# Embedding lookup with positions: indices transposed on VectorE, positions sent without a gate, GpSimd as leader, fewer quarter stores

## The chip, the core and the metric

The kernel runs on one core of a Trainium2 chip. The metric is device time in microseconds (us), the median of several runs. A profile of one execution stands beside it: its span runs from the first to the last instruction of the program, and is some 4 us shorter than the measured time.

The engines that matter here are GpSimd (POOL in the profile), which issues the gathers; VectorE (DVE), which adds; ScalarE (ACT), whose queue issues all plain loads and stores; and the 16 DMA engines that move the data of both. TensorE (PE) has a small part in the kernel before.

## The reference

Each of 32 sequences of 512 indices picks rows of 512 float32 (2 KB) from a table of 50,000 rows, and the row's position vector is added:

```python
batch, seq_len, vocab_size, d_model = 32, 512, 50000, 512

def reference(indices, embedding_table, position_embed):
    token_embed = embedding_table[indices]
    return (token_embed + position_embed).astype(np.float32)
```

The kernel gets the indices as 64-bit integers and uses the lower 32-bit word of each. It reads 33.55 MB of table rows and writes 33.55 MB of output.

## The kernel before

A sequence is laid on 128 partitions with K = 4 positions on each: position 4p + k is on partition p. A gather fetches, for one (sequence b, k), one row for each of 128 partitions, which is 256 KB. There are 128 gathers, and each has one add and a share of a store. Twenty-three slots of SBUF hold a sequence each, so that the first nine are used twice.

```python
P, K, SLOTS, LANES, FIRST, Q = 128, 4, 23, 10, 4, 32     # (shortened)
...
half = K // 2
order = [(b, k) for h in range(2) for b in range(FIRST)
         for k in range(h * half, (h + 1) * half)]
order += [(b, k) for b in range(FIRST, B) for k in range(K)]
stores = []
for g, (b, k) in enumerate(order):
    if (b <= 1 and k < half) or b == B - 1:
        stores.append((g + 1, b, k, 1))
    elif k % half == half - 1:
        stores.append((g + 1, b, k + 1 - half, half))
```

So the first four sequences are gathered in two passes, k = 0 and 1 first, k = 2 and 3 later. A store is a half sequence (512 KB of output), or a quarter (256 KB) for the first halves of sequences 0 and 1 and for all of sequence 31.

ScalarE's queue loads the indices and positions. The indices of sequence 0, of sequences 1 to 3, and of all sequences come in three loads; the second half of the positions is issued only after the first half has landed:

```python
with tc.tile_critical(sync_engine=nc.vector.engine, no_gpsimd_drain=True):


    nc.scalar.dma_start(out=idx0[:, 0, :], in_=idx_first[:, 0, :]).then_inc(
        s_first, 16
    )
    load_pos(0)
    nc.scalar.dma_start(out=idx0[:, 1:, :], in_=idx_first[:, 1:, :]).then_inc(
        s_next, 16
    )
    nc.scalar.dma_start(
        out=idx_raw[:], in_=idx_rows.rearrange("r (s w) -> r s w", w=2)
    ).then_inc(s_raw, 16)
    nc.scalar.wait_ge(s_pos[0], 16)
    load_pos(1)
```

GpSimd builds an identity matrix, waits for the indices of sequence 0 and issues all gathers. From gather 16 on (sequence 4) it takes the indices from `idx_t`, which the preparation below makes. At most LANES = 10 gathers are in flight:

```python
    nc.gpsimd.affine_select(
        out=ident[:], in_=nc.const_aps.tensor(1.0, [P, P], f32),
        pattern=[[-1, P]], compare_op=mybir.AluOpType.is_equal, fill=0.0,
        base=0, channel_multiplier=1,
    ).then_inc(s_prep, 1)
    nc.gpsimd.wait_ge(s_first, 16)
    for g, (b, k) in enumerate(order):
        if g == half:
            nc.gpsimd.wait_ge(s_next, 16)
        if g == FIRST * K:
            nc.gpsimd.wait_ge(s_prep, 2 + K + J)
        if b == SLOTS and k == 0:
            done = sum(1 for x in stores if x[1] in reused)
            nc.gpsimd.wait_ge(s_out, 16 * done)
        if b < FIRST:
            where = idx0[:, b, 2 * k : 2 * k + 1]
        else:
            where = idx_t[:, k, b : b + 1]
        ins = nc.gpsimd.indirect_dma_start(
            out=slots[b % SLOTS][:, k, :],
            out_offset=None,
            in_=table,
            in_offset=bass.IndirectOffsetOnAxis(ap=where, axis=0),
        ).then_inc(s_gather[g % LANES], 16)
        if g >= LANES:
            ins._wait_ge(s_gather[g % LANES], rounds(g - LANES))
    nc.gpsimd.drain()
```

The indices of all sequences lie in memory with 128 consecutive positions to a row of `idx_raw`; they are needed with position 4p + k on partition p. VectorE casts them to float32, TensorE turns them with four transposes into PSUM, and VectorE casts them back with four copies. These stand among the adds, ahead of adds 7 and 9. The positions are copied to PSUM, so that an add has one operand there:

```python
    nc.tensor.wait_ge(s_prep, 2)
    for k in range(K):
        nc.tensor.transpose(
            turned[:, k].rearrange("p b j -> p (b j)"), idx_f[:, :, k], ident[:]
        ).then_inc(s_prep, 1)


    for g, (b, k) in enumerate(order):
        if g == 7:
            nc.vector.tensor_copy(
                out=idx_f[:].rearrange("r p k -> r (p k)"), in_=idx_raw[:, :, 0]
            )._wait_ge(s_raw, 16).then_inc(s_prep, 1)
        if g == 9:
            nc.vector.wait_ge(s_prep, 2 + K)
            for j in range(J):
                nc.vector.tensor_copy(
                    out=idx_t[j * Q : (j + 1) * Q, :, :], in_=turned[:, :, :, j]
                ).then_inc(s_prep, 1)
        if b == 0:
            nc.vector.tensor_copy(out=pos_ps[:, k, :], in_=pos_sb[:, k, :])._wait_ge(
                s_pos[k // half], 16
            ).then_inc(s_ps, 1)
            nc.vector.wait_ge(s_ps, k + 1)
        part = slots[b % SLOTS][:, k, :]
        nc.vector.tensor_tensor(
            out=part, in0=part, in1=pos_ps[:, k, :], op=add
        )._wait_ge(s_gather[g % LANES], rounds(g)).then_inc(s_add, 1)


    rest = 0
    for adds, b, at, n in stores:
        done = s_out if b in reused else s_rest
        rest += b not in reused
        nc.scalar.dma_start(
            out=out_rows[b][:, at : at + n, :],
            in_=slots[b % SLOTS][:, at : at + n, :],
        )._wait_ge(s_add, adds).then_inc(done, 16)
tc.no_sync_barrier()
nc.scalar.wait_ge(s_rest, nc.scalar.to_reg(16 * rest))
```

Of the kernel before, what the change touches and what calls it, by code (L numbers as in the profile page):

```python
# [7 lines left out]
P = 128  # L8
K = 4
SLOTS = 23  # L10
LANES = 10
FIRST = 4
Q = 32


@with_exitstack
def kernel(
    ctx: ExitStack,
    tc: tile.TileContext,
    indices: bass.AP,  # L20
    embedding_table: bass.AP,
    position_embed: bass.AP,
    out: bass.AP,
):

    nc = tc.nc
    f32 = mybir.dt.float32
    i32 = mybir.dt.int32
    add = mybir.AluOpType.add

    B, S = indices.shape
    V, D = embedding_table.shape
    assert S == P * K and B == 32
    assert V < (1 << 24), "an index passes through float32"
    J = P // Q  # L40


    idx_words = indices.bitcast(i32)
    idx_first = idx_words[0:FIRST].rearrange("b (p w) -> p b w", p=P)
    idx_rows = idx_words.rearrange("b (j w) -> (b j) w", j=J)
    out_rows = out.rearrange("b (p k) d -> b p k d", k=K)
    pos_rows = position_embed.rearrange("(p k) d -> p k d", k=K)
    table = embedding_table[:, :]

    def sbuf(name, shape, dtype):  # L50
        return ctx.enter_context(tc.tile_pool(name="p_" + name, bufs=1)).tile(
            shape, dtype, name=name
        )

    def psum(name, shape, dtype):
        pool = tc.tile_pool(name="p_" + name, bufs=1, space=bass.MemoryType.PSUM)
        return ctx.enter_context(pool).tile(shape, dtype, name=name)

    idx0 = sbuf("idx0", [P, FIRST, 2 * K], i32)
    idx_raw = sbuf("idx_raw", [P, Q * K, 2], i32)  # L60
    ident = sbuf("ident", [P, P], f32)
    idx_f = sbuf("idx_f", [P, Q, K], f32)
    idx_t = sbuf("idx_t", [P, K, B], i32)
    pos_sb = sbuf("pos_sb", [P, K, D], f32)
    slots = [sbuf(f"slot{n}", [P, K, D], f32) for n in range(SLOTS)]
    turned = psum("turned", [Q, K, B, J], f32)
    pos_ps = psum("pos_ps", [P, K, D], f32)


# [4 lines that stand above are left out]
    order += [(b, k) for b in range(FIRST, B) for k in range(K)]  # L74
    stores = []
    for g, (b, k) in enumerate(order):
        if (b <= 1 and k < half) or b == B - 1:
            stores.append((g + 1, b, k, 1))
        elif k % half == half - 1:
            stores.append((g + 1, b, k + 1 - half, half))  # L80

    sem = tc.alloc_semaphore
    s_first, s_next, s_raw = sem("s_first"), sem("s_next"), sem("s_raw")
    s_pos = [sem(f"s_pos{h}") for h in range(2)]
    s_gather = [sem(f"s_gather{n}") for n in range(LANES)]

    reused = range(B - SLOTS)
    s_out, s_rest = sem("s_out"), sem("s_rest")

    s_prep, s_ps, s_add = sem("s_prep"), sem("s_ps"), sem("s_add")  # L90

    def rounds(g):
        return 16 * (g // LANES + 1)

    def load_pos(h):
        part = slice(h * half, (h + 1) * half)
        nc.scalar.dma_start(out=pos_sb[:, part, :], in_=pos_rows[:, part, :]).then_inc(
            s_pos[h], 16
        )

    with tc.tile_critical(sync_engine=nc.vector.engine, no_gpsimd_drain=True):  # L101


        nc.scalar.dma_start(out=idx0[:, 0, :], in_=idx_first[:, 0, :]).then_inc(
            s_first, 16
        )
        load_pos(0)
        nc.scalar.dma_start(out=idx0[:, 1:, :], in_=idx_first[:, 1:, :]).then_inc(
            s_next, 16
        )  # L110
        nc.scalar.dma_start(
            out=idx_raw[:], in_=idx_rows.rearrange("r (s w) -> r s w", w=2)
        ).then_inc(s_raw, 16)
        nc.scalar.wait_ge(s_pos[0], 16)
        load_pos(1)


        nc.gpsimd.affine_select(  # L118
            out=ident[:], in_=nc.const_aps.tensor(1.0, [P, P], f32),
            pattern=[[-1, P]], compare_op=mybir.AluOpType.is_equal, fill=0.0,  # L120
            base=0, channel_multiplier=1,
        ).then_inc(s_prep, 1)
        nc.gpsimd.wait_ge(s_first, 16)
        for g, (b, k) in enumerate(order):
            if g == half:
                nc.gpsimd.wait_ge(s_next, 16)
            if g == FIRST * K:
                nc.gpsimd.wait_ge(s_prep, 2 + K + J)
            if b == SLOTS and k == 0:
                done = sum(1 for x in stores if x[1] in reused)  # L130
                nc.gpsimd.wait_ge(s_out, 16 * done)
            if b < FIRST:
                where = idx0[:, b, 2 * k : 2 * k + 1]
            else:
                where = idx_t[:, k, b : b + 1]
            ins = nc.gpsimd.indirect_dma_start(  # L136
# [7 lines that stand above are left out]
        nc.gpsimd.drain()  # L144


        nc.tensor.wait_ge(s_prep, 2)
        for k in range(K):
            nc.tensor.transpose(  # L149
                turned[:, k].rearrange("p b j -> p (b j)"), idx_f[:, :, k], ident[:]  # L150
            ).then_inc(s_prep, 1)


        for g, (b, k) in enumerate(order):
            if g == 7:
                nc.vector.tensor_copy(  # L156
                    out=idx_f[:].rearrange("r p k -> r (p k)"), in_=idx_raw[:, :, 0]
                )._wait_ge(s_raw, 16).then_inc(s_prep, 1)
            if g == 9:
                nc.vector.wait_ge(s_prep, 2 + K)  # L160
                for j in range(J):
                    nc.vector.tensor_copy(  # L162
                        out=idx_t[j * Q : (j + 1) * Q, :, :], in_=turned[:, :, :, j]
                    ).then_inc(s_prep, 1)
            if b == 0:
                nc.vector.tensor_copy(out=pos_ps[:, k, :], in_=pos_sb[:, k, :])._wait_ge(  # L166
                    s_pos[k // half], 16
# [18 lines that stand above are left out]
# [30 lines left out]
```

## Time and profile before

| | before |
|---|---|
| median of 3 runs | 181.71 us (181.65 to 181.85) |
| span of the profile | 178.1 us |
| GpSimd busy | 121.8 us (68%), 133 instructions |
| VectorE busy | 91.4 us (51%), 137 instructions |
| TensorE busy | 1.0 us |
| moved by DMA | 68.34 MB, mean 384 GB/s |
| gathers, as a share of 16 DMA engines | 48.1% |
| loads and stores, likewise | 48.6% |
| one gather issued by GpSimd | 0.95 us |
| one add, 128x512 float32 | 687 ns |

Busy time is time in which an engine works; the rest it waits or has nothing to do. In a chain of waits, "issue" is time in which an engine waited for nothing that the profile shows. "Releaser" is what ended a wait. A DMA's landing is the moment its completion is seen. The share of the DMA engines is the mean over 16 of them, and packets that overlap count in full, so that it can be a little over 1.

The profile lists, for one gather on GpSimd, only its issue; when its data is there is read from the add that waits for it.

### The profile page before, as it was taken

The numbers are of one execution on the slowest core, as the hardware profiler recorded it, in microseconds if no ns is written. First come the engines' busy times: TensorE is split into PE (matmuls) and PEld (weight loads), VectorE is DVE, ScalarE is ACT, GpSimd is POOL, SyncE is SP. The second block draws the span as 40 slices with busy tenths as digits, with TensorE's granted clock in tenths as the row PEclk, the third lists the DMA queues.
The fourth block names the chain that finished last, engine by engine and source line by source line (L and its number), as shares of the span: only waits on it lengthen the run. The fifth ranks groups of instructions, "written<-read, shape, count | busy, mean of one in ns | idle before, by whom it ended". The sixth has DMA issues, their size and how long they took to land.

```text
span 178.1 us, 415 instructions
## 1 busy us (share of the span) xinstructions
PE 1.0 (1%) x4; PEld 0.4 (0%) x4; DVE 91.4 (51%) x137; POOL 121.8 (68%) x133
## 2 busy tenths in 40 slices
PE   0000100000000000000000000000000000000000
PEld 0000000000000000000000000000000000000000
DVE  0445973455556555555556455555556555554510
POOL 3777777777777777777777777777777777774000
DMA  4899999999999999999999999999999999999960
GB/s 122 234 329 359 375 378 364 385 410 413 416 416 419 419 419 420 419 420 419 419 420 420 419 419 418 419 418 419 420 419 420 418 420 420 420 419 421 417 258 0
DMA packets 21011, 68.34 MB, mean 384 GB/s; under 512 B 3728, under 2 KB 3856, under 8 KB 21008
## 3 DMA queue, kind: packets, MB, share of 16 engines
q10 hardware_dynamic: 10768, 34.76, 48.6%
q0 software_dynamic: 10240, 33.56, 48.1%
q14 instruction: 3, 0.02, 0.0%
HBM read 34.75 MB, written 33.55 MB: 384 GB/s over the span
## 4 chain that ended last, share of the span: by engine, by line
POOL 65%; issue 23%; DMA 5%; DVE 2%; ACTq 0%; DVEq 0%
POOL slot L136 65%; DMA slot<-in_embedding_table_dram,idx_t 4%; DVE slot L171 2%; DMA idx<-in_indices_dram 1%; ACTq L211 0%; DVEq L101 0%
## 5 line engine op out<-in xcount | busy, mean ns | idle before, releaser
L136 POOL DMA_INDIRECT slot<-in_embedding_table_dram,idx_t x112 | 106.0, 946 | 34.1 <-issue 34.1
L171 DVE TENSOR_TENSOR slot<-slot,pos_ps 128x512 f32<-128x512 f32 x128 | 87.7, 687 | 73.8 <-issue 57.8
L136 POOL DMA_INDIRECT slot<-in_embedding_table_dram,idx x16 | 15.3, 958 | 6.0 <-issue 4.6
L166 DVE COPY pos_ps<-pos_sb 128x512 f32<-128x512 f32 x4 | 2.7, 685 | 4.9 <-DMA pos_sb<-in_position_embed_dram 4.9
L162 DVE CAST idx_t<-turned 32x128 int32<-32x128 f32 x4 | 1.1, 280 | 0.1
L149 PE MATMUL turned<-ident,idx_f 128*32 128x128 f32 x4 | 1.0, 413 | 17.6 <-issue 17.6
L118 POOL TENSOR_SCALAR_AFFINE_SELECT ident<-const-float32-1.0 128x128 f32<-128x128 f32 x1 | 0.3, 282 | 0.7 <-DVEq L101 0.7
L149 PEld LDWEIGHTS turned<-ident,idx_f 128*32 128x32 f32 x4 | 0.4, 131 | 17.7 <-issue 17.6
L200 POOL MEMSET const-float32-0.0<- 128x1 f32 x1 | 0.1, 99 | 0.3 <-issue 0.3
L156 DVE CAST idx_f<-idx_raw 128x128 f32<-128x128 int32 x1 | 0.2, 220 | 0.0
L200 POOL MEMSET const-uint8-127<- 128x1 uint8 x1 | 0.1, 116 | 0.0
L200 POOL MEMSET const-bfloat16-1.0<- 128x1 bf16 x1 | 0.1, 110 | 0.0
L200 POOL MEMSET const-float32-1.0<- 128x1 f32 x1 | 0.1, 102 | 0.0
## 6 DMA issues: line engine op xcount, KB each, us to landing
out_dram<-slot ACTq DMA_DIRECT2D x60, 512.0 KB
out_dram<-slot ACTq DMA_DIRECT2D x8, 256.0 KB
slot<-in_embedding_table_dram,idx_t POOLq DMA_INDIRECT x112
pos_sb<-in_position_embed_dram ACTq DMA_DIRECT2D x2, 512.0 KB, 4.7
slot<-in_embedding_table_dram,idx POOLq DMA_INDIRECT x16
idx_raw<-in_indices_dram ACTq DMA_DIRECT2D x1, 128.0 KB
idx<-in_indices_dram ACTq DMA_DIRECT2D x1, 4.0 KB, 1.6
idx<-in_indices_dram ACTq DMA_DIRECT2D x1, 12.0 KB
```

The lines of the kernel that those rows point to most:

```text
L118: nc.gpsimd.affine_select(out=ident[:], in_=nc.const_aps.tensor(1.0, [P, P], f32), pattern=[[-1, P]], compare_op=mybir.AluOpType.is_equal, ...
L136: ins = nc.gpsimd.indirect_dma_start(out=slots[b % SLOTS][:, k, :], out_offset=None, in_=table, in_offset=bass.IndirectOffsetOnAxis(ap=whe ...
L149: nc.tensor.transpose(turned[:, k].rearrange("p b j -> p (b j)"), idx_f[:, :, k], ident[:]).then_inc(s_prep, 1)
L156: nc.vector.tensor_copy(out=idx_f[:].rearrange("r p k -> r (p k)"), in_=idx_raw[:, :, 0])._wait_ge(s_raw, 16).then_inc(s_prep, 1)
L162: nc.vector.tensor_copy(out=idx_t[j * Q : (j + 1) * Q, :, :], in_=turned[:, :, :, j]).then_inc(s_prep, 1)
L166: nc.vector.tensor_copy(out=pos_ps[:, k, :], in_=pos_sb[:, k, :])._wait_ge(s_pos[k // half], 16).then_inc(s_ps, 1)
L171: nc.vector.tensor_tensor(out=part, in0=part, in1=pos_ps[:, k, :], op=add)._wait_ge(s_gather[g % LANES], rounds(g)).then_inc(s_add, 1)
L200: nc = _bacc.Bacc("TRN2", target_bir_lowering=False, num_devices=1)
```

## The change

It has five parts.

1. The indices are transposed by VectorE itself, in squares of 32, as the first thing that VectorE does. The identity, the casts and TensorE's transposes go. For this the indices are loaded in four parts, each to 32 partitions, so that after the transposition of each square a position is on its partition.
2. `idx0` holds the indices of sequence 0 alone; the load for sequences 1 to 3 goes. GpSimd takes the transposed indices from gather 2 on (`g == half`), where before it took them from gather 16.
3. The second half of the positions is issued without waiting for the first.
4. The critical section is led by GpSimd instead of VectorE. The leader signals the other engines at its start and collects them at its end.
5. Quarter stores remain only for the first half of sequence 0 and the second half of sequence 31: there are 4 instead of 8, and 66 stores instead of 68.

It is meant to make the preparation of the indices shorter and simpler, to have the positions sooner, and to have fewer small transfers.

The diff, cut to its core:

```diff
-    idx_first = idx_words[0:FIRST].rearrange("b (p w) -> p b w", p=P)
-    idx_rows = idx_words.rearrange("b (j w) -> (b j) w", j=J)
+    idx_first = idx_words[0].rearrange("(p w) -> p w", p=P)
+    idx_rows = idx_words.rearrange("b (j w) -> b j w", j=J)
...
-    idx0 = sbuf("idx0", [P, FIRST, 2 * K], i32)
-    idx_raw = sbuf("idx_raw", [P, Q * K, 2], i32)
-    ident = sbuf("ident", [P, P], f32)
-    idx_f = sbuf("idx_f", [P, Q, K], f32)
+    idx0 = sbuf("idx0", [P, 2 * K], i32)
+    idx_raw = sbuf("idx_raw", [P, 2 * Q * K], i32)
...
-        if (b <= 1 and k < half) or b == B - 1:
+        if (b == 0 and k < half) or (b == B - 1 and k >= half):
             stores.append((g + 1, b, k, 1))
...
-    with tc.tile_critical(sync_engine=nc.vector.engine, no_gpsimd_drain=True):
+    with tc.tile_critical(sync_engine=nc.gpsimd.engine, no_gpsimd_drain=True):
-        nc.scalar.dma_start(out=idx0[:, 0, :], in_=idx_first[:, 0, :]).then_inc(
-            s_first, 16
-        )
+        nc.scalar.dma_start(out=idx0[:, :], in_=idx_first).then_inc(s_first, 16)
         load_pos(0)
-        nc.scalar.dma_start(out=idx0[:, 1:, :], in_=idx_first[:, 1:, :]).then_inc(
-            s_next, 16
-        )
-        nc.scalar.dma_start(
-            out=idx_raw[:], in_=idx_rows.rearrange("r (s w) -> r s w", w=2)
-        ).then_inc(s_raw, 16)
-        nc.scalar.wait_ge(s_pos[0], 16)
+        for j in range(J):
+            nc.scalar.dma_start(
+                out=idx_raw[j * B : (j + 1) * B, :], in_=idx_rows[:, j, :]
+            ).then_inc(s_raw, 16)
         load_pos(1)
...
-        nc.gpsimd.affine_select(
...
         nc.gpsimd.wait_ge(s_first, 16)
         for g, (b, k) in enumerate(order):
             if g == half:
-                nc.gpsimd.wait_ge(s_next, 16)
-            if g == FIRST * K:
-                nc.gpsimd.wait_ge(s_prep, 2 + K + J)
+                nc.gpsimd.wait_ge(s_idx, 1)
...
-            if b < FIRST:
-                where = idx0[:, b, 2 * k : 2 * k + 1]
+            if g < half:
+                where = idx0[:, 2 * k : 2 * k + 1]
             else:
                 where = idx_t[:, k, b : b + 1]
...
-        nc.tensor.wait_ge(s_prep, 2)
-        for k in range(K):
-            nc.tensor.transpose(
...
+        nc.vector.transpose(
+            out=idx_t[:],
+            in_=idx_raw[:].rearrange("r (q k w) -> r k q w", k=K, w=2)[:, :, :, 0],
+        )._wait_ge(s_raw, 16 * J).then_inc(s_idx, 1)
         for g, (b, k) in enumerate(order):
-            if g == 7:
-                nc.vector.tensor_copy(
-                    out=idx_f[:].rearrange("r p k -> r (p k)"), in_=idx_raw[:, :, 0]
-                )._wait_ge(s_raw, 16).then_inc(s_prep, 1)
-            if g == 9:
-                nc.vector.wait_ge(s_prep, 2 + K)
-                for j in range(J):
-                    nc.vector.tensor_copy(
-                        out=idx_t[j * Q : (j + 1) * Q, :, :], in_=turned[:, :, :, j]
-                    ).then_inc(s_prep, 1)
```

More of the change, by code (lines that the diff above doesn't have):

```diff
@@ L38 @@
     assert S == P * K and B == 32
-    assert V < (1 << 24), "an index passes through float32"
     J = P // Q
+    assert B == Q, "indices are turned in squares of 32"
     idx_words = indices.bitcast(i32)
-    idx_first = idx_words[0:FIRST].rearrange("b (p w) -> p b w", p=P)
-    idx_rows = idx_words.rearrange("b (j w) -> (b j) w", j=J)
+    idx_first = idx_words[0].rearrange("(p w) -> p w", p=P)
+    idx_rows = idx_words.rearrange("b (j w) -> b j w", j=J)
     out_rows = out.rearrange("b (p k) d -> b p k d", k=K)
@@ L65 @@
     slots = [sbuf(f"slot{n}", [P, K, D], f32) for n in range(SLOTS)]
-    turned = psum("turned", [Q, K, B, J], f32)
     pos_ps = psum("pos_ps", [P, K, D], f32)
@@ L82 @@
     sem = tc.alloc_semaphore
-    s_first, s_next, s_raw = sem("s_first"), sem("s_next"), sem("s_raw")
+    s_first, s_raw, s_idx = sem("s_first"), sem("s_raw"), sem("s_idx")
     s_pos = [sem(f"s_pos{h}") for h in range(2)]
@@ L88 @@
     s_out, s_rest = sem("s_out"), sem("s_rest")
-    s_prep, s_ps, s_add = sem("s_prep"), sem("s_ps"), sem("s_add")
+    s_ps, s_add = sem("s_ps"), sem("s_add")
     def rounds(g):
@@ L99, in load_pos @@
         )
-    with tc.tile_critical(sync_engine=nc.vector.engine, no_gpsimd_drain=True):
-        nc.scalar.dma_start(out=idx0[:, 0, :], in_=idx_first[:, 0, :]).then_inc(
-            s_first, 16
-        )
+    with tc.tile_critical(sync_engine=nc.gpsimd.engine, no_gpsimd_drain=True):
+        nc.scalar.dma_start(out=idx0[:, :], in_=idx_first).then_inc(s_first, 16)
         load_pos(0)
-        nc.scalar.dma_start(out=idx0[:, 1:, :], in_=idx_first[:, 1:, :]).then_inc(
-            s_next, 16
-        )
-        nc.scalar.dma_start(
-            out=idx_raw[:], in_=idx_rows.rearrange("r (s w) -> r s w", w=2)
-        ).then_inc(s_raw, 16)
-        nc.scalar.wait_ge(s_pos[0], 16)
-        load_pos(1)
-        nc.gpsimd.affine_select(
-            out=ident[:], in_=nc.const_aps.tensor(1.0, [P, P], f32),
-            pattern=[[-1, P]], compare_op=mybir.AluOpType.is_equal, fill=0.0,
-            base=0, channel_multiplier=1,
-        ).then_inc(s_prep, 1)
+        for j in range(J):
+            nc.scalar.dma_start(
+                out=idx_raw[j * B : (j + 1) * B, :], in_=idx_rows[:, j, :]
+            ).then_inc(s_raw, 16)
+        load_pos(1)
         nc.gpsimd.wait_ge(s_first, 16)
@@ L144 @@
         nc.gpsimd.drain()
-        nc.tensor.wait_ge(s_prep, 2)
-        for k in range(K):
-            nc.tensor.transpose(
-                turned[:, k].rearrange("p b j -> p (b j)"), idx_f[:, :, k], ident[:]
-            ).then_inc(s_prep, 1)
-        for g, (b, k) in enumerate(order):
-            if g == 7:
-                nc.vector.tensor_copy(
-                    out=idx_f[:].rearrange("r p k -> r (p k)"), in_=idx_raw[:, :, 0]
-                )._wait_ge(s_raw, 16).then_inc(s_prep, 1)
-            if g == 9:
-                nc.vector.wait_ge(s_prep, 2 + K)
-                for j in range(J):
-                    nc.vector.tensor_copy(
-                        out=idx_t[j * Q : (j + 1) * Q, :, :], in_=turned[:, :, :, j]
-                    ).then_inc(s_prep, 1)
+        nc.vector.transpose(
+            out=idx_t[:],
+            in_=idx_raw[:].rearrange("r (q k w) -> r k q w", k=K, w=2)[:, :, :, 0],
+        )._wait_ge(s_raw, 16 * J).then_inc(s_idx, 1)
+        for g, (b, k) in enumerate(order):
             if b == 0:
```

## The prediction

> **What bounds the kernel now.** I first read the page's share of busy time (GpSimd 68%, VectorE 51%) and its DMA row, then the same span cut into stretches, because a kernel that starts empty and ends empty has stages with different limits. In these rows the last three numbers are the granted clock, the mean busy share of the 16 DMA engines and GB/s.
>
> ```profile
> 2.00:4.00 2.00, 0.00 (x0) 0.00 (x0) 0.00 (x0) 1.11 (x1) 1.00 0.72 215
> 4.00:6.00 2.00, 0.00 (x0) 0.00 (x0) 0.69 (x1) 1.39 (x3) 1.00 0.94 250
> 6.00:10.00 4.00, 0.00 (x0) 0.00 (x0) 1.29 (x2) 3.09 (x4) 1.00 0.85 223
> 10.00:15.00 5.00, 0.00 (x0) 0.00 (x0) 2.81 (x5) 3.78 (x5) 1.00 0.95 356
> 15.00:40.00 25.00, 1.04 (x4) 0.43 (x4) 14.82 (x26) 18.91 (x21) 1.00 1.01 381
> 40.00:160.00 120.00, 0.00 (x0) 0.00 (x0) 65.87 (x97) 90.75 (x97) 1.00 1.03 418
> 160.00:170.00 10.00, 0.00 (x0) 0.00 (x0) 5.64 (x9) 2.28 (x3) 1.00 1.03 418
> ...
> 171.00:173.10 2.10, 0.00 (x0) 0.00 (x0) 0.00 (x0) 0.00 (x0) 1.00 0.53 203
> 173.10:178.10 5.00, 0.00 (x0) 0.00 (x0) 0.00 (x0) 0.00 (x0) 1.00 0.00 0
> ```
>
> From 40 to 170 us the DMA engines are full: share 1.03, 418 GB/s, also after GpSimd has issued its last gather at 162.9 us. So the transfers are a bound. GpSimd is a second one of the same size. The chain of waits shows it issuing a gather every 1.25 us (0.95 us of work and 0.30 us of "issue"), from the second gather on and without one longer gap:
>
> ```profile
> 4.33 0.95 POOL slot L136
> 5.28 0.30 issue
> 5.59 0.95 POOL slot L136
> 6.54 0.30 issue
> ```
>
> 128 such steps are 160 us, from 2.89 to 162.9. A step asks for 256 KB of gather and 256 KB of store, 524,288 bytes in 1.25 us or 419 GB/s, which is what the engines move. The time from a gather's end on GpSimd to its add on VectorE tells how far the DMA engines are behind: 2.6 us for the first gather (4.03 to 6.67 us in the timeline), 6.7 us for the last (162.89 to 169.59). That queue of some 4 us was built in the first 40 us and is never worked off. So a gain can only come from the two ends: DMA engines that idle early (shares 0.72 to 0.95 up to 15 us), and the last microseconds, where the share is 0.53. The 5 us after the last byte are program end.
>
> **What the skill says.** The Trainium skill, "DMA: Bandwidth & Descriptors", section "Queues, rings and completion order", says that each DMA engine takes its queues in turn, a packet at a time. The trace agrees: gathers (q0) and the other transfers (q10) hold 48.1% and 48.6%. So positions sent early share with gathers and don't shut them out. "VectorE: DVE Perf Modes", section "The three transpose paths", says that VectorE transposes 32x32 blocks, 311 ns for 128x128 bf16. No transpose of this kind runs before, so the trace can't confirm it; my estimate for 128x128 int32 is 0.25 to 0.4 us, from that figure and the cast of equal shape at 220 ns in this profile. "DMA: Bandwidth & Descriptors", section "Anatomy of one DMA — SWDGE (gpsimd) path", says that most of a transfer's fixed cost is its completion; here the first 4 KB of indices took 1.58 us from issue to landing.
>
> **The change, part by part.**
>
> 1. *Index preparation.* Removed from VectorE: one cast of 220 ns and four of 280 ns, 1.3 us in all, which with their waits stand between 17.30 and 21.07 us among the adds; from TensorE four transposes; from GpSimd the identity (0.28 us, before its first wait, so off the path). Added: one transpose, 0.3 us, before any position copy. The removed VectorE work delayed some stores near 22 us by about 1.4 us, when the store queue was thin; that may be worth 0.1 to 0.2 us of DMA filling, no more, as VectorE is only half busy.
>
> 2. *An earlier need.* Gather 2 now needs the transposed indices; before, gather 16 was the first. All 128 KB of indices must land, be transposed and release GpSimd. Before, positions' first half was in by 4.93 us (the copy starts then), and the packet records put the last index packets (1,024 B) at 5.45 us. They were issued at 2.41 us, behind 384 packets of 32 B that now go. ScalarE now issues four index transfers from 1.93 us at about 0.45 us each, the last at 3.3 to 3.8; a transfer's first packet came about 1.0 us after its issue, so 4.3 to 4.8 us, still close behind the positions. I take landing at 5.2 us, transpose to 5.6, and 0.3 us to GpSimd's start (the first gather started 0.28 us after its indices landed): gather 2 at 5.9 instead of 5.59. All later gathers move by that 0.3 us. While the DMA engines have a queue, this costs nothing; as they idle partly here, I charge 0.1 us.
>
> 3. *Positions ungated.* The second 512 KB are issued at about 3.8 us instead of 4.93, as the wait for the first half goes. The DMA engines then have them at about 5 us. They were least busy just there: 0.60 between 6 and 7 us in a finer cut. One microsecond earlier for 512 KB that need 1.3 us at full rate; idle share is 0.15 x 4 us = 0.6 us between 6 and 10 us and 0.25 us from 10 to 15. I count on half of that and a little: 0.5 us. The rest will not be filled, because the first store can't come before the first add, and gather 0 shares the engines with the positions, so that this add may be some tenths later.
>
> 4. *Fewer small packets.* 384 packets of 32 B at 9 ns on 16 engines: 0.2 us, of which half lay in an idle stretch, so 0.1. Four quarter stores become two halves. In the packet records a quarter is 128 packets of 2,048 B at 84 ns, a half 128 of 4,096 B at 159 ns: per engine 16 x 84 = 1,344 ns against 8 x 159 = 1,272 ns. With one completion less, 80 ns a pair, 0.16 us for both. The half of sequence 1 is issued after the fourth add, when the second quarter was; store data still waited in the queue then. Likewise the half of sequence 31 at 167.97 us, when the queue reached to 169.3. No delay from either.
>
> 5. *GpSimd leads.* At the start the leader's signal changes hands, from VectorE at 0.83 us to GpSimd; all engines were released together, so nothing. At the end there is one odd row:
>
> ```profile
> 169.59 0.69 DVE L171 TENSOR_TENSOR slot<-slot,pos_ps 128x512 f32<-128x512 f32 x1 [0.27 <-issue]
> 171.10 0.34 ACTq L180 DMA_DIRECT2D out_dram<-slot  x1
> ```
>
> The last add ends at 170.28, but its store is issued at 171.10, 0.8 us later; the store before followed its add within 0.03 us (169.33 to 169.36), as the others do. VectorE, as the leader, has its closing drain queued directly behind this add from 169.72 us. If that drain holds back the add's signal, then GpSimd as leader frees it: the store's data would follow the one before and fill the share of 0.53 in 171 to 173.1 us, about 0.75 us sooner. I give this even chances: 0.35 us.
>
> **Sum.** -0.15 (VectorE) +0.1 (gather 2) -0.5 (positions) -0.1 -0.16 (packets) -0.35 (end) = -1.2 us. These gains overlap: engines filled earlier by positions can't be filled again by stores. And what the DMA engines gain early shortens the queue, not GpSimd's 160 us, so it shows only because the queue of 4 us remains at the end. I take three quarters: -0.9, so 181.71 - 0.9 = 180.8 us.
>
> **Rivals.** (a) *GpSimd's pace is the true bound and the new wait moves it.* For it: the unbroken 1.25 us steps; the chain of waits puts 65% on GpSimd. Against it: the queue of 4 us behind it at the end, which takes up a delay. If indices land at 6.5 us, behind positions or late issues, gather 2 starts near 7.2, 1.6 us late. The queue shrinks, yet with idle engines in between perhaps 0.6 us is lost, and the result is about 181.7 to 182.2. (b) *The positions are hidden anyway, or get in the way.* Sent earlier they delay gather 0, the first add and first store by their 1.3 us, and the idle time moves from 6 us to 9 us. For it: the first add waits for gather 0 alone, and adds feed stores. Against it: before, store 0 was issued at 7.39 but had to queue behind the same positions. Then only packets and end remain: about 181.2. (c) *The end is freed in full and positions fill well:* 0.75 + 0.8 + 0.3 gives 180.0 or a little less.
>
> **Range and chances.** (c) and (a) set the ends: 179.9 to 181.8. Nothing touches the 120 us in the middle, where bytes and rate are the same, so 2% (3.6 us) either way would need both ends to change by more than they hold: faster by over 2%: 0.03, slower: 0.02, within: 0.95. I hold a small gain for much likelier than a small loss, about 4 to 1.
>
> **What would show it.** In the changed profile: gather 2 on GpSimd between 5.7 and 6.3 us, with a wait on VectorE's transpose ahead of it; the transpose at 0.25 to 0.4 us; DMA share from 6 to 10 us above 0.9; 418 GB/s in the middle as before; gather to add at the end 6 us or less instead of 6.7; the last store within 0.1 us of the last add. It is wrong if gather 2 starts after 7 us, if the steps of 1.25 us lengthen, or if the last store is still 0.8 us late.

## The result: 1.3% slower

| | before | after |
|---|---|---|
| median | 181.68 us (4 runs, 181.65 to 181.85) | 183.99 us (4 runs, 183.55 to 184.92) |
| ratio to before | | 1.013 (95% interval 1.009 to 1.018) |
| span of the profile | 178.1 us | 179.9 us |
| gather 2 starts | 5.59 us | 7.10 us |
| GpSimd's last gather issued | 162.89 us | 164.28 us |
| last add ends | 170.28 us | 172.24 us |

The changed kernel cut into the stretches used before (VectorE and GpSimd busy, with their counts; then clock, DMA share, GB/s):

```profile
2.00:4.00 2.00, 0.00 (x0) 1.08 (x1) 1.00 0.79 254
4.00:6.00 2.00, 0.00 (x0) 0.95 (x1) 1.00 0.81 149
6.00:10.00 4.00, 2.61 (x5) 2.29 (x3) 1.00 0.80 291
10.00:15.00 5.00, 1.75 (x3) 3.78 (x5) 1.00 0.81 218
15.00:40.00 25.00, 14.27 (x22) 18.91 (x21) 1.00 1.01 384
40.00:160.00 120.00, 65.18 (x95) 90.76 (x97) 1.00 1.03 415
160.00:170.00 10.00, 5.50 (x8) 3.37 (x4) 1.00 1.03 417
170.00:173.10 3.10, 1.38 (x2) 0.00 (x0) 1.00 1.02 413
173.10:174.70 1.60, 0.00 (x0) 0.00 (x0) 1.00 0.67 255
```

The middle is as full as before (share 1.03), at 415 GB/s instead of 418. The start is uneven: 10 to 15 us fell from 356 to 218 GB/s and 4 to 6 us from 250 to 149, while 2 to 4 us rose from 215 to 254 and 6 to 10 us from 223 to 291. The timeline of the changed kernel's start says what GpSimd did there; the bracket at the end of a row is the idle time of the engine and what ended it:

```profile
1.79 1.87 ACTq L102 DMA_DIRECT2D idx_raw<-in_indices_dram  x4
2.80 1.08 POOL L119 DMA_INDIRECT slot<-in_embedding_table_dram,idx  x1 [2.35 <-DMA idx<-in_indices_dram]
...
4.19 0.95 POOL L119 DMA_INDIRECT slot<-in_embedding_table_dram,idx  x1 [0.30 <-issue]
6.43 0.41 DVE L130 STREAM_TRANSPOSE idx_t<-idx_raw 128x128 int32<-128x128 int32 x1 [6.43 <-DMA idx_raw<-in_indices_dram]
...
7.10 0.94 POOL L119 DMA_INDIRECT slot<-in_embedding_table_dram,idx_t  x1 [1.97 <-DVE idx_t L130]
8.23 0.69 DVE L141 TENSOR_TENSOR slot<-slot,pos_ps 128x512 f32<-128x512 f32 x1 [0.81 <-DMA slot<-in_embedding_table_dram,idx]
```

VectorE waits until 6.43 us for the indices and transposes in 0.41 us; GpSimd sits idle 1.97 us instead of 0.30 and starts gather 2 at 7.10. From there its steps are 1.25 us as before, so that it ends 1.4 us later. The chain of waits of the changed kernel puts the same stretch on the index load:

```profile
3.22 3.19 DMA idx_raw<-in_indices_dram
6.40 0.02 issue
6.43 0.42 DVE idx_t L130
6.84 0.26 issue
7.10 0.94 POOL slot L119
```

At the end, the queue in the DMA engines has not shrunk: from the last gather's end to its add it is 7.27 us (164.28 to 171.55), before it was 6.71. GpSimd is late, and the DMA engines are late with it. The last store now follows the last add at once:

```profile
171.55 0.69 DVE L141 TENSOR_TENSOR slot<-slot,pos_ps 128x512 f32<-128x512 f32 x1 [0.48 <-issue]
172.28 0.34 ACTq L150 DMA_DIRECT2D out_dram<-slot  x1
```

### The profile page after: what moved, and what is told of

Its sections match the earlier page's. It is cut to its first block, busy times and chain, and to the rows that moved or that the text cites. A ratio compares the mean times of both kernels' runs of the same rounds, so it can differ in the third digit from the quotient of the medians.

```text
span 179.9 us, 395 instructions
## 1 busy us (share of the span) xinstructions
DVE 90.7 (50%) x133; POOL 121.3 (67%) x132
## 3 DMA queue, kind: packets, MB, share of 16 engines
q0 software_dynamic: 10240, 33.56, 48.6%
## 4 chain that ended last, share of the span: by engine, by line
POOL 64%; issue 22%; DMA 6%; DVE 1%; ACTq 1%; POOLq 1%
POOL slot L119 64%; DMA slot<-in_embedding_table_dram,idx_t 4%; DMA idx_raw<-in_indices_dram 2%; DVE slot L141 1%; ACTq L102 1%; POOLq L127 1%; ACTq L93 0%; DVE idx_t L130 0%; ACTq L99 0%; ACTq L181 0%; POOLq L97 0%; POOLq L170 0%
## 5 line engine op out<-in xcount | busy, mean ns | idle before, releaser
L119 POOL DMA_INDIRECT slot<-in_embedding_table_dram,idx_t x126 | 119.1, 945 | 40.0 <-issue 38.1
L119 POOL DMA_INDIRECT slot<-in_embedding_table_dram,idx x2 | 2.0, 1014 | 2.7 <-DMA idx<-in_indices_dram 2.4
```

Source lines behind the costliest of these rows:

```text
L119: ins = nc.gpsimd.indirect_dma_start(out=slots[b % SLOTS][:, k, :], out_offset=None, in_=table, in_offset=bass.IndirectOffsetOnAxis(ap=whe ...
```

## The experiments

Three theories went in. **A**: gather 2 waits for all indices, and GpSimd's delay is paid. **B**: the positions sent early take the DMA engines from the first gathers. **C**: the middle is slower (415 against 418 GB/s) for another reason, such as the places of the buffers. The kernel before takes 176.3 to 182.5 us in the sessions of these runs (chip 9 had 182.47 us in one and 176.61 in another). The difference follows the last byte or lies outside the span: 5.3 and 4.3 us in e7, 1.3 and 1.7 us in e1. So each ratio is to the kernel before in the same session; it need not be the quotient of the two medians, from which it differs by up to 0.3%. All experiments carry one line that the two kernels don't have, behind ScalarE's closing wait: `nc.scalar.sem_inc(s_ps, 1)`.

The control, with that line alone:

> The changed kernel, with one more semaphore increment on ScalarE behind its closing wait, which all these experiments carry. Every theory expects the changed kernel's time within 0.3 us: 183.6 to 184.5 us, gather 2 at about 7.1 us, last store issued within 0.1 us of the last add.

Measured: 178.65 us against 176.30, ratio 1.013 (1.011 to 1.015). Gather 2 started at 7.50 us. The line costs nothing that shows.

**Late need.** In the changed kernel:

```diff
+        # (cut: idx0 holds sequences 0 to 3 again; 1 to 3 are loaded behind the first positions)
             if g == half:
+                nc.gpsimd.wait_ge(s_next, 16)
+            if g == FIRST * K:
                 nc.gpsimd.wait_ge(s_idx, 1)
```

> The changed kernel, but the indices of sequences 1 to 3 are loaded apart again and GpSimd needs the transposed ones only at gather 16. Theory A (the wait of gather 2 for all indices is what costs: GpSimd's steps start 1.5 us late and nothing takes that up): gather 2 back at 5.5 us, time down by about 2 us or more, to 181 to 182 us. Theory B (the positions sent early take the DMA engines from the first gathers): at most 0.5 us less, above 183.2 us. Theory C (the rate in the middle is lower, 415 instead of 418 GB/s, for another reason such as the layout of the buffers): above 183 us, 415 GB/s again.

Measured: 175.89 us, ratio 0.997 (0.996 to 0.999); gather 2 at 5.59 us, 418 GB/s in the middle:

```profile
5.59 0.94 POOL L123 DMA_INDIRECT slot<-in_embedding_table_dram,idx  x1 [0.41 <-DMA idx<-in_indices_dram]
```

The loss is gone, though here VectorE's transpose ended only at 8.6 us and the first add began at 9.32. In this run the early gather counted and the late add did not. (The larger `idx0` also puts the later buffers back on their old places; that is taken apart below.)

**Gate.** In the changed kernel, `nc.scalar.wait_ge(s_pos[0], 16)` ahead of `load_pos(1)` again:

> The changed kernel, but the second half of the positions waits for the first again. Theory A: gather 2 still at about 7 us and the time within 0.5 us of the changed kernel. Theory B: the DMA share between 10 and 15 us goes from 0.81 to 0.95, and the time falls by 1.5 to 2 us. Theory C: no change.

Measured: 177.33 us, ratio 1.005 (1.004 to 1.007); gather 2 at 7.07 us, a share of 0.91 from 10 to 15 us. Between A and B: the gate wins back 1.3 of 2.35 us, and 1.0 us stays.

**Indices first.** In the changed kernel:

```diff
-        load_pos(0)
         for j in range(J):
             nc.scalar.dma_start(... idx_raw ...)
+        load_pos(0)
         load_pos(1)
```

> The changed kernel, but the four index loads are issued ahead of both halves of the positions, so that no position packet and no gather packet stands ahead of an index packet. Theory A: indices land before 4.5 us, the transpose ends before 5.2, gather 2 starts at about 5.5 without a wait, and the time falls by about 2 us to 181 to 182 us, as in the run with the late need. Theory B: positions come still later and next to the first gathers, so no gain: 183.5 us or more. Theory C: no gain.

Measured: 176.26 us, ratio 1.001 (0.999 to 1.002). Its timeline:

```profile
1.32 1.87 ACTq L101 DMA_DIRECT2D idx_raw<-in_indices_dram  x4
...
4.16 0.95 POOL L119 DMA_INDIRECT slot<-in_embedding_table_dram,idx  x1 [0.30 <-issue]
4.49 0.41 DVE L130 STREAM_TRANSPOSE idx_t<-idx_raw 128x128 int32<-128x128 int32 x1 [4.49 <-DMA idx_raw<-in_indices_dram]
5.41 0.95 POOL L119 DMA_INDIRECT slot<-in_embedding_table_dram,idx_t  x1 [0.30 <-issue]
```

The transpose is over at 4.90 us, and gather 2 has no wait but its usual 0.30 us. The order of two loads removes 2.4 us, with the early need, the ungated positions and the new places of the buffers all kept. This speaks for A, against B and C as causes that act alone.

**A pure delay.** In the kernel before, ahead of gather 2, five or ten identity matrices into a buffer that nobody reads:

```diff
             if g == half:
                 nc.gpsimd.wait_ge(s_next, 16)
+                for n in range(5):          # and 10
+                    nc.gpsimd.affine_select(out=scratch[:, n, :], ...)
```

> The kernel before, nothing of the change in it, but GpSimd makes five identity matrices (0.28 us each in the profile before, into a buffer nobody reads) between gather 1 and gather 2: some 1.4 to 1.6 us of pure delay, with index loads, positions and stores as before. Theory A in its hard form (GpSimd's delay is paid in full): 1.2 to 1.9 us above the kernel before. Prediction's own view (the queue of 4 us in the DMA engines takes it up): less than 0.4 us above. Theory B alone also expects less than 0.4 us.

> The same with ten matrices, some 3 us of delay. Paid in full: 2.6 to 3.6 us above the kernel before. Taken up by the queue: less than 1 us. If a first part is free and the rest is paid, this run is above by more than twice what five matrices cost.

Measured: 183.47 and 184.35 us against 182.47, ratios 1.006 (1.004 to 1.008) and 1.011 (1.009 to 1.014). The timeline with five:

```profile
5.34 1.26 POOL L129 TENSOR_SCALAR_AFFINE_SELECT scratch<-const-float32-1.0 128x128 f32<-128x128 f32 x5
6.57 0.69 DVE L178 TENSOR_TENSOR slot<-slot,pos_ps 128x512 f32<-128x512 f32 x1 [1.19 <-DMA slot<-in_embedding_table_dram,idx]
6.76 0.98 POOL L143 DMA_INDIRECT slot<-in_embedding_table_dram,idx  x1 [0.16 <-issue]
```

Gather 2 started 1.17 us late (6.76 against 5.59), and the medians are 1.00 us apart (1.1 us by the ratio); with ten, it is 2.39 us late (7.98) and 1.88 (2.1) us are paid. So 0.8 to 0.95 us for each microsecond, from the first one on; the intervals leave 0.6 to 1.3 with five and 0.7 to 1.0 with ten. The matrices took 0.25 us each, less than the expectation's 0.28, so that its bounds in us were too high. The prediction's own view (less than 0.4 us and less than 1 us) is out, as the intervals begin at 0.7 and 1.7 us; the queue takes up a small part at most.

**GpSimd leads, alone.** In the kernel before, `sync_engine=nc.gpsimd.engine`:

> The kernel before with GpSimd instead of VectorE as the leader, nothing else. If the closing drain behind the last add held back its signal: the last store follows its add within 0.1 us instead of 0.8, and the time falls by 0.4 to 0.8 us. If the 0.8 us had another cause, or lies beside other transfers: no change beyond 0.2 us.

Measured: 182.29 us against 182.47, ratio 1.000 (0.998 to 1.001). No gain, though the last store follows at once (170.22 to 170.25 us).

**The rest of the change.** In the changed kernel: late need, the gate, and the transpose among the adds (`if g == 7:` ahead of it):

> All of the change that does not touch the early indices or the positions: transpose on VectorE but placed among the adds ahead of add 7, the first four sequences from their own index loads (first need at gather 16), positions gated as before, GpSimd as leader, four quarter stores. Theory A: gather 2 at about 5.5 us; the end gains its 0.4 to 0.8 us and the packets 0.1 to 0.3, so 0.5 to 1.1 us below the kernel before. If only the changed kernel's delay counts and the end is no gain: within 0.2 us of the kernel before.

Measured: 182.45 us against 182.47, ratio 1.001 (1.000 to 1.002). VectorE's transpose in place of five casts and TensorE, the leader and the four quarter stores less are together worth nothing that shows; the gain of 0.5 us or more that the expectation allowed did not come. The 384 packets of 32 B are still in this run.

**The places of the buffers.** A side effect that the diff doesn't show: `idx0` shrank from 128 to 32 B a partition, and every later buffer moved by it. The raw indices, the positions and the slots then start 160 B past a multiple of 256 B instead of on one. In the packet records some 15 to 20% of the 4,096 B packets then take longer than 159 ns between 40 and 160 us, in the kernels with the old places 0.1 to 1%. The runs that bear on it, e9 and e10 on one chip, f1 to f4 on another:

```diff
# e9, f3: changed kernel with idx0 at its old size (e10: and the index loads ahead of the positions)
-    idx0 = sbuf("idx0", [P, 2 * K], i32)
+    idx0 = sbuf("idx0", [P, FIRST * 2 * K], i32)
# f1: kernel before with 160 B of unused space behind idx0
-    idx0 = sbuf("idx0", [P, FIRST, 2 * K], i32)
+    idx0 = sbuf("idx0", [P, FIRST * 2 * K + 40], i32)[:, : FIRST * 2 * K].rearrange(...)
# f4: changed kernel with 96 B of unused space behind idx_t
-    idx_t = sbuf("idx_t", [P, K, B], i32)
+    idx_t = sbuf("idx_t", [P, K * B + 24], i32)[:, : K * B].rearrange(...)
```

> The changed kernel with nothing moved in time, but the tile of sequence 0's indices keeps its old size of 128 B a partition (it shrank to 32 B, which moved every later buffer by 96 B, so that the slots start at 32 past a multiple of 64 B instead of on one). Theory C (this offset makes packets of 4,096 B jitter: 20% of them take longer than 159 ns in the profiles with the offset, under 1% in those without): the rate between 40 and 160 us back to 418 GB/s and 0.4 to 1.0 us less than the changed kernel. Theories A and B: no change beyond 0.3 us.

> The changed kernel with both: old size of that tile, and the index loads ahead of the positions. Theory A alone: like the run with indices first, within 0.3 us of the kernel before. A with C: 0.4 to 0.8 us better than that, so 0.3 to 0.8 us below the kernel before.

> The kernel before, with 160 B of unused space after the tile of the first indices: nothing is moved in time, but pos_sb and the slots start 160 B past a multiple of 256 B, as in the changed kernel, instead of on one. Theory C (the offset by itself costs): packets jitter (a fifth above 159 ns), rate between 40 and 160 us 415 to 417 GB/s, and 0.6 to 1.8 us above the kernel before. If the offset only costs together with the early need of gather 2: within 0.4 us of the kernel before.

> The changed kernel once more (with the closing increment), beside the two below on the same chip: 1.0 to 1.5% above the kernel before, gather 2 at 7.0 us or later.

> The changed kernel with the old tile size once more. If the offset is worth about 1% of the 1.3%: 0.2 to 0.5% above the kernel before, gather 2 near 6.2 us as in the first profile. If the first result was a difference of chips: 1% or more above it, gather 2 at 7.0 us or later.

> The changed kernel with the unused space after idx_t: positions and slots start where they do in the run with the old tile size, but the raw indices keep their offset of 32 B. If the offset of the slots is what costs: the same as the run with the old tile size. If the offset of the raw indices makes their load land late: gather 2 at 7.0 us or later and 0.8% or more above the kernel before.

| run | ratio to before (95% interval) | gather 2 | packets over 159 ns |
|---|---|---|---|
| old size (e9) | 1.003 (1.001 to 1.005) | 6.18 us | 1% |
| old size, indices first (e10) | 0.999 (0.997 to 1.001) | 5.41 us | 1% |
| before with the offset (f1) | 1.000 (0.998 to 1.002) | 5.60 us | 20% |
| control again (f2) | 1.014 (1.010 to 1.017) | 7.35 us | 17% |
| old size again (f3) | 1.008 (1.006 to 1.010) | 7.20 us | 1% |
| slots alone on old places (f4) | 1.010 (1.006 to 1.014) | 7.38 us | 1% |

The first of these looked like a find: 1.003 instead of 1.013. But its indices had landed early in the profiled execution, and on the next chip the same kernel had gather 2 at 7.20 us and 1.008. The ratios of e9 and f3 leave out runs that lie over 1.5% above the kernel's fastest, three and four of 22; with these the quotients of the means are 1.005 and 1.009. The offset by itself costs nothing that shows (f1, within 0.2%), although packets take longer. Whether it adds some tenths of a per cent beside a late gather 2 can't be told from the times: the intervals of f2, f3 and f4 overlap, if only just. The middle hints at it: from 40 to 160 us the five profiles with both the new places and gather 2 at 6.97 us or later (changed kernel, e1, e3, f2, g1) have 415 to 416 GB/s, the other fifteen 417 to 419. No run tests why.

**Positions ungated, alone and with a punctual gather 2.** The gate taken out of the kernel before (e12), and out of the run with late need and gate (e11, and again g2):

> The run with the late need and the gate, but positions ungated. If positions sent early only cost when gather 2 is late (nothing then fills the DMA engines between 8 and 11 us): here they cost nothing or gain, 0 to 0.6 us below the kernel before. If they cost by themselves (theory B): 0.8 to 1.3 us above it.

> The kernel before with the gate taken out, nothing else: the part of the change alone. The prediction counted on 0.5 us less. Theory B: 0.8 to 1.3 us more. Theory A, with positions harmful only beside a late gather 2: between no change and 0.5 us less.

> The changed kernel with the gate on the positions, once more: its first profile fell on the slowest of its runs. If the gate helps by filling the DMA engines between 8 and 10 us: 0.4 to 0.7% above the kernel before with gather 2 still at 6.9 us or later, and a share above 0.7 between 8 and 10 us (0.51 in the control). If it helps by letting the indices land sooner: gather 2 at 6.6 us or earlier.

> The version that was fastest so far (need of the transposed indices at gather 16, positions ungated, transpose among the adds) once more on another chip: 0.1 to 0.4% below the kernel before, gather 2 at 5.4 to 5.6 us.

Measured: e12 176.42 us against 176.31, ratio 1.001 (0.999 to 1.002), no gain. e11 0.997 (0.996 to 0.999), g2 0.996 (0.995 to 0.998) on another chip: with e2 (0.997) the fastest version of this study, below both kernels. The gate in the changed kernel again (g1): 1.006 (1.003 to 1.008), gather 2 at 6.97 us. The stretch from 8 to 10 us, first in the control, then with the gate:

```profile
8.00:10.00 2.00, 1.37 (x3) 1.39 (x3) 1.00 0.51 164
```

```profile
8.00:10.00 2.00, 1.38 (x3) 1.48 (x2) 1.00 0.76 231
```

With the gate the second positions come later and fill these two microseconds. Ungated they end at 8.65 us in the changed kernel's packet records and its first store's packets begin at 10.47 us. Between them only gather 1 (to 9.38 us), gather 2 (from 8.79 us) and the first of gather 3 move. With late need and ungated (e2) gather 2 was issued at 5.59 us, and the same stretch is full:

```profile
8.00:10.00 2.00, 1.67 (x4) 1.60 (x2) 1.00 0.90 318
```

So in these runs positions sent early harm only beside a late gather 2. That the empty stretch is what costs the 1.3 us is argued, not shown: the control's profile is of its fastest run and g1's is not, and these two runs lie 1.6 and 1.2 us above the median of the kernel before, only 0.4 us apart. The rest of the 1.3 us is in runs without a profile.

## Why the prediction was wrong

**The bound.** Both bounds were read rightly: steps of 1.25 us in every profile, 415 to 419 GB/s in every middle. What was concluded from them was wrong. "While the DMA engines have a queue, this costs nothing" treats the queue as a store to draw on. When gather 2 is due, at 5.6 us, it is only being built: in the kernel before, the time from a gather's end to its add is 2.6 us for gather 0, 5.2 for gather 8 and 7.0 from gather 28 on, at some 40 us. Later it isn't drawn on either. In all twenty profiles GpSimd's steps from gather 3 on are 1.25 us (1.26 at most), so its last gather is late by about what gather 2 was, and the add of that last gather follows after 6.0 to 7.5 us where gather 2 is late, after 6.5 to 7.7 us where it is not. As both sides run at the same rate, neither catches up. What the DMA engines haven't moved in the first 40 us they move later at some 418 GB/s. The view by stretches shows this account, first before, then after:

```profile
0.00:40.00 40.00, 1.04 (x4) 0.43 (x4) 19.62 (x33) 28.76 (x35) 1.00 0.92 328
```

```profile
0.00:40.00 40.00, 18.62 (x29) 27.21 (x33) 1.00 0.89 317
```

For nine of the profiles:

| profile | gather 2, us | GB/s, 0 to 40 us | profiled run above the median of before, us |
|---|---|---|---|
| indices first (e4) | 5.41 | 332 | -0.6 |
| best again (g2) | 5.43 | 331 | -0.8 |
| GpSimd leads (e7) | 5.75 | 328 | -0.1 |
| old size (e9) | 6.18 | 325 | 0.3 |
| delay of five (e5) | 6.76 | 320 | 0.9 |
| gate again (g1) | 6.97 | 317 | 1.2 |
| changed kernel | 7.10 | 317 | 1.9 |
| control again (f2) | 7.35 | 311 | 1.5 |
| delay of ten (e6) | 7.98 | 302 | 2.0 |

All eleven profiles with gather 2 up to 6.2 us have 324 to 332 GB/s and lie -0.8 to 0.6 us from that median; the nine with a later gather 2 have 302 to 320 GB/s and lie 0.8 to 2.0 us above it.

Eleven GB/s less over 40 us (328 before, 317 after) are 0.44 MB, at 418 GB/s 1.1 us; the rate of 415 in the middle, 0.36 MB in 120 us, makes 0.9 us more. Together that is 1.9 of the 2.0 us by which the changed kernel's last add is later. The delay alone does not slow the middle (418 and 417 GB/s in e5 and e6), so the cause of these 0.9 us stays open.

**Step 2, the early need, is the one that failed, twice over.** It put the indices' landing at 5.2 us, gather 2 at 5.9, and charged 0.1 us. The start was 7.10: the packet records have the last index packet ending at 5.57 us, the load's last completion write at 6.08, and VectorE starting at 6.43. The estimate of 5.2 us lay below even the 5.45 us that the records before showed, and left the completion out. The Trainium skill, "DMA: Bandwidth & Descriptors", section "Anatomy of one DMA — SWDGE (gpsimd) path", says for transfers that GpSimd issues that completion is most of the fixed cost. These loads are issued by ScalarE, and the trace decides: for the first 4 KB of indices in the kernel before, 1.0 of the 1.58 us lie before the first packet and 0.3 us after the last; for this load it is 0.86 us from last byte to use. The records show the first gather's packets among the last of the indices, taking up to 1.4 us each, where 159 ns is usual later. With the load ahead of everything (e4), its last packet ended at 4.11 us, before those packets came, and VectorE started 0.38 us later. The four completions by themselves are thus not the cause, as e4 has them too. That the gather's packets are the cause is read from the records; no run took them apart from the positions ahead of the load. The price was wrong too: 0.8 to 0.95 us a microsecond, not 0.3. For 1.5 us late that is 1.2 to 1.4 us of the 2.3; with the gate, where gather 2 was as late, 1.0 us stayed.

**Step 3, positions ungated**, was put at 0.5 us of gain. Alone it is nothing (e12). Beside the late gather 2 it costs what the gate wins back, 0.8% or 1.3 us (1.013 against 1.005 and 1.006). All four pairs have been run: gather 2 punctual and gated 1.001 (e8), punctual and ungated 0.996 to 1.001, late and gated 1.005 and 1.006, late and ungated 1.013 and 1.014 (1.008 and 1.010 with the slots on their old places, where no late and gated run of the changed kernel stands beside them). The prediction judged each part on the schedule of the kernel before, in which gathers followed each other without the gap that the other part made. The share from 6 to 10 us was to rise above 0.9 and was 0.80. The equal shares of 48.1% and 48.6%, read as a sign that the queues are served in turn, follow from the equal bytes of the two (33.56 and 34.76 MB) and don't show how they share at the start. Beside the late need it may gain some 0.3% (e8 against e11 and g2, in different sessions); why it does there and not in the kernel before stays open.

**Steps 1, 4 and 5** were put at 0.15, 0.26 and 0.35 us of gain; together they are none that shows (e8: 1.001, 1.000 to 1.002), without the 0.1 us for the 384 packets, which no run tests alone. The transpose took 406 ns, just above the estimate. Step 5 was hung on one row: the last store 0.8 us after its add. With VectorE still the leader, it follows at once in the other profiles, as here with the delay of five:

```profile
170.05 0.69 DVE L178 TENSOR_TENSOR slot<-slot,pos_ps 128x512 f32<-128x512 f32 x1 [0.46 <-issue]
170.77 0.34 ACTq L187 DMA_DIRECT2D out_dram<-slot  x1
```

So the 0.8 us belonged to that execution and not to the leader; what made it is not known.

**The rivals.** (a) named the mechanism: indices near 6.5 us, gather 2 near 7.2. It priced it at the same cheap rate and so ended at 181.7 to 182.2 instead of 184. (b) named the second part, idle time that moves from 6 to 9 us, but as a gain that fails to come, not as a cost. The two were set side by side as alternatives and came together.

## What to carry to other kernels

Where the engine that issues transfers and the engines that move them run at the same rate, a queue between them is no slack: here GpSimd's delay at the start stayed to the end, nearly in full. Before work is made to wait for more data at the start, follow that data's last packet, its completion and the next engine's start one by one, and put the load ahead of the bulk that it would stand behind. Judge parts of a change together: a transfer moved forward fills a gap or opens one, depending on what else has moved.

## What was not expected of the hardware

In the first 40 us single gather packets take up to 1.6 us (2.3 us in the kernel before, 1.4 to 2.5 us over all profiles); between 40 and 160 us 80% or more of the packets of 4,096 B take at most 159 ns. This happens in every profile and keeps the rate at 360 to 395 GB/s between 15 and 40 us although the share is 1.0.

With buffers 160 B past a multiple of 256 B, 15 to 20% of the 4,096 B packets take longer than 159 ns. It shows in those of the stores, on the mean 159.7 ns (f1) instead of 159.1 (e12); the means of the gathers' packets overlap (159.6 to 161.3 ns with the offset, 159.2 to 160.8 without). The Trainium skill, "DMA: Bandwidth & Descriptors", section "How a descriptor splits into AXI transactions", says that a descriptor that doesn't start on 256 B costs more beats; the trace agrees in direction, with 0.4%, and the kernel's time didn't change (f1: 1.000).
